# Fused matmul and row RMS norm on one core: the first loads reordered around the table load, the first moves split over two engines, eight warm matmuls instead of eleven

## The chip, the cores and the metric

The kernel runs on one core of a Trainium2 chip. The metric is the time of one execution in device microseconds, lower is better. "Span" is the time from the first to the last instruction in the profile; it is about 1.8 us less than the reported time.

The engines are called TensorE (PE in the profile, PEld for its weight loads), VectorE (DVE), ScalarE (ACT), GpSimd (POOL) and SyncE (SP). A "q" after the name (ACTq) is the engine's sequencer, which issues instructions and DMAs.

## The reference

```python
m, k, n = 2048, 2048, 2048          # a: [m, k], b: [k, n], gamma: [n], all float32

def reference(a, b, gamma, eps):
    x = np.matmul(a, b)
    rms = np.sqrt(np.mean(x ** 2, axis=-1, keepdims=True) + eps)
    return (gamma * x / rms).astype(np.float32)
```

## The kernel before

The contraction has 16 tiles of 128 rows, handled as eight pairs (kp = 0 to 7). In its head, the kernel forms the first four row blocks (HB = 4) times the left half of B, pair by pair: for each pair it needs a piece of A (512 rows by 256 columns) and a tile of B (256 rows by 1024 columns). Pair 0 comes as float32 on the two hardware DMA queues (SyncE and ScalarE) and is cast on the engines. Pairs 1 to 7 come through the software queue, which GpSimd feeds and which casts to bf16 on the way.

```python
    # pair 0, float32, on the hardware queues
    nc.sync.dma_start(out=a0f, in_=a[0:HB * P, 0:W2].rearrange("(r p) k -> p r k", p=P))
    for t in range(2):
        nc.scalar.dma_start(out=b0f[t], in_=b[t * P:(t + 1) * P, 0:HALF])
    # ... cut ...
    def load_head(kp):            # one pair through the software queue: A's piece, then B's tile
        nc.gpsimd.dma_start(out=ah(kp), in_=a[0:HB * P, kp * W2:(kp + 1) * W2].rearrange(...))
        load_b(0, kp)
    load_head(1)
    identity_f = consts.tile([P, P], FP32, name="identity_f")
    make_identity(nc, identity_f)
    for kp in range(2, 4):
        load_head(kp)
    # ... cut ...
    # warm matmuls: of zeros, only to keep TensorE busy until data is there
    warm_bank = ps_a.tile([P, CH], FP32, name="acc")
    for _ in range(11):
        nc.tensor.matmul(warm_bank, warm[:, 0:P], warm[:, 0:CH], start=True, stop=True)
    # ... cut ...
    def transpose_first():        # pair 0: transpose A on TensorE, move it out of PSUM, cast B
        bank = [ps_t.tile([P, CH], FP32, name="tbank"), ps_a.tile([P, CH], FP32, name="acc")]
        view = [b.rearrange("p (r m) -> p r m", r=HB) for b in bank]
        for t in range(2):
            for r in range(HB):
                nc.tensor.matmul(view[t][:, r, :], a0f[:, r, t * P:(t + 1) * P], identity_f,
                                 is_transpose=True, start=(r == 0), stop=(r == HB - 1))
        for t in range(2):
            cast_first = [lambda: nc.vector.tensor_copy(out=raw[0][0][:, t, :CH],
                                                        in_=b0f[t][:, :CH]),
                          lambda: nc.scalar.copy(out=raw[0][0][:, t, CH:], in_=b0f[t][:, CH:])]
            move = [lambda h=h: nc.vector.tensor_copy(
                out=head_at[:, t, 2 * h:2 * h + 2, :], in_=view[t][:, 2 * h:2 * h + 2, :])
                for h in range(2)]
            for work in (cast_first + move if t == 0 else move + cast_first):
                work()
```

After that each pair is 7 + 7 matmuls of 128x512, 8 transposes for the next pair and 2 matmuls into a separate bank. The rest of the kernel (right half of B, then Strassen products for the other row blocks, the norms and the stores) is not touched by the change.

## Time and profile before

| | before |
|---|---|
| time | 224.43 us, median of 3 (224.06 to 224.67) |
| span of the profiled run | 222.6 us |
| TensorE, busy share of the span | 95% |
| first matmul of pair 0 | 7.71 us |
| first matmul of pair 1 | 12.38 us |
| first matmul of pair 4 | 24.69 us |

First, the chain that ended last, from the profile's page of the kernel before: the shares of the span by engine.

```profile
PE 83%; DMA 8%; DVE 2%; POOL 2%; issue 1%; ACT 1%; DVEq 0%; ACTq 0%; POOLq 0%
```

The same chain in order of time (start us, us, what), where it passes from loads to TensorE:

```profile
6.53 0.65 POOL early L106
7.18 17.47 DMA b<-in_b_dram
24.64 0.04 issue
24.69 1.67 PE acc L350 x7
```

From 24.69 us on, the chain is TensorE until 209.5 us. What holds the start of that stretch is a load: B's tile for pair 4, issued at 7.18 us and landed at 24.64.

Next, lines of the timeline of the kernel before (start us, us of busy time, engine, line, operation, out<-in, count, and in brackets the idle time before it and what ended it):

```profile
0.74 0.46 SPq L92 DMA_DIRECT2D early<-in_a_dram  x1
0.75 0.91 ACTq L94 DMA_DIRECT2D early<-in_b_dram  x2
1.46 3.92 PE L138 MATMUL acc<-sq 128*128 128x512 bf16 x11 [1.46 <-DVE sq L129]
1.69 1.28 ACT L153 ACT_TABLE_LOAD   x1 [1.69 <-PEq L718]
...
5.14 0.73 DVE L151 CAST b<-early 128x512 bf16<-128x512 f32 x1 [1.32 <-DMA early<-in_b_dram]
...
6.57 0.63 PE L148 MATMUL tbank<-identity_f,early 128*128 128x128 f32 x4 [1.18 <-POOL msq L198]
7.23 0.76 DVE L154 CAST head_at<-tbank 128x256 bf16<-128x256 f32 x2 [1.36 <-PE tbank L148]
7.71 2.76 PE L350 MATMUL acc<-b,head_at 128*128 128x512 bf16 x12
10.31 0.61 PE L165 MATMUL tbank<-identity,early 128*128 128x128 bf16 x8
...
23.65 0.59 PE L382 MATMUL tbank<-b,head_at 128*128 128x512 bf16 x2
24.69 1.67 PE L350 MATMUL acc<-b,head_at 128*128 128x512 bf16 x7 [0.44 <-DMA b<-in_b_dram]
```

- VectorE casts B's first tile at 5.14 us, *before* A has landed. When the transposes are done, at 7.2, only the move out of PSUM is left, and the first matmul follows 0.48 us after the move starts.

- The last pair of lines shows slack. From pair 1 on, the two matmuls into the separate bank (L382) are followed 0.43 us later by the next pair, except before pair 4. There TensorE would have been ready at 23.65 + 0.43 = 24.08 us, and waited until 24.69: 0.6 us.

The landing records in the trace (a load is complete with its sixteenth increment, one from each DMA engine) suggest why: of pair 4's tile fifteen parts had landed by 23.68 us and the sixteenth at 24.64, 0.96 us later. A 16 KB packet of the instruction queue started at 21.38 us and took 0.97 us.

### The profile page before, as it was taken

The numbers are of one execution on the slowest core, as the hardware profiler recorded it, in microseconds if no ns is written. First come the engines' busy times: TensorE is split into PE (matmuls) and PEld (weight loads), VectorE is DVE, ScalarE is ACT, GpSimd is POOL, SyncE is SP. The second block draws the span as 40 slices with busy tenths as digits, with TensorE's granted clock in tenths as the row PEclk, the third lists the DMA queues.
The fourth block names the chain that finished last, engine by engine and source line by source line (L and its number), as shares of the span: only waits on it lengthen the run. The fifth ranks groups of instructions, "written<-read, shape, count | busy, mean of one in ns | idle before, by whom it ended". The sixth has DMA issues, their size and how long they took to land.

```text
span 222.6 us, 3026 instructions
## 1 busy us (share of the span) xinstructions
PE 211.1 (95%) x1043; PEld 98.6 (44%) x1043; DVE 161.8 (73%) x324; ACT 129.1 (58%) x272; POOL 24.5 (11%) x49
## 2 busy tenths in 40 slices
PE   7899999999999999999999999999999999999950
PEld 2445444444454444444444444444444444444430
DVE  2427557983999989978949298837994589587692
ACT  3110002807698895799646985699478954334570
POOL 7534232300000001000100002000200000000000
PEclk9999999999999999999999999999999999999997
DMA  6999999999973499818889259945994794044045
GB/s 184 223 202 209 203 208 211 212 303 259 327 280 159 188 272 292 310 72 226 276 228 400 58 174 222 366 151 143 246 368 168 97 282 189 0 188 193 0 190 188
DMA packets 36176, 47.13 MB, mean 212 GB/s; under 512 B 21952, under 2 KB 26048, under 8 KB 34496
## 3 DMA queue, kind: packets, MB, share of 16 engines
q0 software_dynamic: 9648, 23.33, 41.6%
q1 hardware_dynamic: 26080, 22.29, 33.0%
q10 hardware_dynamic: 432, 1.31, 2.0%
q8 instruction: 8, 0.13, 0.2%
q14 instruction: 8, 0.07, 0.1%
HBM read 34.60 MB, written 16.78 MB: 231 GB/s over the span
## 4 chain that ended last, share of the span: by engine, by line
PE 83%; DMA 8%; DVE 2%; POOL 2%; issue 1%; ACT 1%; DVEq 0%; ACTq 0%; POOLq 0%
PE acc L279 63%; PE acc L350 18%; DMA b<-in_b_dram 8%; POOL early L106 1%; DVE x L617 1%; POOL b L100 1%; DVE x L620 1%; PE tbank L179 1%; PE tbank L382 1%; PE tbank L165 1%; ACT sq L291 0%; DVEq L732 0%; ACT sq L682 0%; DVE x L690 0%; DVE r L322 0%
## 5 line engine op out<-in xcount | busy, mean ns | idle before, releaser
L279 PE MATMUL acc<-b,s 128*128 128x512 bf16 x376 | 83.3, 379 | 0.0
L279 PEld LDWEIGHTS <-s 128*128 128x128 f16 x472 | 46.2, 98 | 55.7 <-DVE s L244 0.2
L350 PE MATMUL acc<-b,head_at 128*128 128x512 bf16 x240 | 55.1, 379 | 0.6 <-DMA b<-in_b_dram 0.4
L291 ACT ACTIVATE sq<-x 128x512 bf16<-128x512 f32 x62 | 39.1, 631 | 10.9 <-DVE x L520 5.1
L340 DVE SCALAR_TENSOR_TENSOR x<-x,r,gamma_sb 128x1024 f32<-128x1024 f32 x28 | 34.7, 1282 | 0.8
L209 ACT ACTIVATE sq<-a 128x1024 bf16<-128x1024 f32 x24 | 25.4, 1057 | 16.8 <-DMA a<-in_a_dram 16.4
L350 PEld LDWEIGHTS <-head_at 128*128 128x128 bf16 x240 | 22.9, 98 | 26.7 <-issue 1.1
L393 ACT COPY x<-acc 128x512 f32<-128x512 f32 x11 | 5.9, 591 | 25.1 <-PE acc L350 25.1
L231 ACT ACTIVATE head_at<-a,s 128x2048 f16<-128x2048 f32 x10 | 19.9, 1990 | 0.0
L279 PEld LDWEIGHTS <-at_even 128*128 128x128 f16 x96 | 9.4, 98 | 11.5 <-issue 0.4
L279 PEld LDWEIGHTS <-head_at 128*128 128x128 f16 x96 | 9.4, 98 | 11.3
L100 POOL DMA_DIRECT2D b<-in_b_dram x15 | 10.6, 708 | 16.0 <-DMA b<-in_b_dram 13.2
L217 DVE TENSOR_SCALAR s<-norm 128x1 f32<-128x1 f32 x12 | 1.8, 150 | 14.3 <-ACT norm L212 14.2
L244 DVE TENSOR_TENSOR s<-at_even 128x1024 f16<-128x1024 f16 x15 | 9.7, 684 | 2.8 <-DMA at_even<-head_at 2.8
L291 ACT ACTIVATION_READ_ACCUMULATOR sq<-x 128x1 f32 x62 | 11.7, 188 | 0.0
L279 PE MATMUL acc<-t_left,s 128*128 128x512 bf16 x48 | 11.3, 379 | 0.0
L279 PE MATMUL acc<-early,s 128*128 128x512 bf16 x48 | 11.3, 379 | 0.0
L279 PE MATMUL acc<-early,at_even 128*128 128x512 bf16 x48 | 11.0, 379 | 0.0
L279 PE MATMUL acc<-t_left,at_even 128*128 128x512 bf16 x48 | 10.9, 379 | 0.0
L509 ACT COPY x<-acc 128x512 f32<-128x512 f32 x10 | 5.7, 575 | 8.9 <-PE acc L279 8.9
L279 PE MATMUL acc<-t_left,head_at 128*128 128x512 bf16 x48 | 10.8, 379 | 0.0
L279 PE MATMUL acc<-early,head_at 128*128 128x512 bf16 x48 | 10.8, 379 | 0.0
(86 smaller groups left out, 205.8 us busy)
## 6 DMA issues: line engine op xcount, KB each, us to landing
out_dram<-x SPq DMA_DIRECT2D x30, 512.0 KB, 3.1
a<-in_a_dram POOLq DMA_DIRECT2D x12, 1024.0 KB, 8.5
b<-in_b_dram POOLq DMA_DIRECT2D x15, 512.0 KB, 17.1
early<-in_a_dram POOLq DMA_DIRECT2D x7, 256.0 KB, 14.8
early<-in_b_dram ACTq DMA_DIRECT2D x2, 512.0 KB, 5.9
gamma_sb<-in_gamma_dram POOLq DMA_DIRECT2D x1, 1024.0 KB, 19.9
out_dram<-x SPq DMA_DIRECT2D x3, 256.0 KB, 3.5
early<-in_a_dram SPq DMA_DIRECT2D x1, 512.0 KB, 5.7
```

The source lines that it names most:

```text
L100: nc.gpsimd.dma_start(out=raw[j][kp], in_=b[kp * W2:(kp + 1) * W2, j * HALF:(j + 1) * HALF].rearrange("(t p) n -> p t n", p=P))
L106: nc.gpsimd.dma_start(out=ah(kp), in_=a[0:HB * P, kp * W2:(kp + 1) * W2].rearrange("(r p) k -> p r k", p=P))
L165: nc.tensor.matmul(view[:, t, r, :], ah(kp)[:, r, t * P:(t + 1) * P], identity, is_transpose=True, start=(t == 0 and r == 0), stop=(t == 1 ...
L209: nc.scalar.activation(out=junk, in_=a32[mb][:, h * HALF:(h + 1) * HALF], func=ACTF.Square, scale=2.0 ** -8, accum_out=n2[:, h:h + 1])
L231: nc.scalar.activation(out=a16[mb], in_=a32.pop(mb), func=ACTF.Copy, scale=factor.pop(mb))
L244: nc.vector.tensor_tensor(out=s_sum[s], in0=x, in1=y, op=op)
L279: nc.tensor.matmul(bank, lhsT[:, kp, :], rhs, start=(start and kp == 0), stop=(kp == KP - 1), skip_group_check=not start)
L291: nc.scalar.activation(out=sq[:, 0:CH], in_=src, func=ACTF.Square, scale=inv_sqrt_n, accum_out=msq[mb][:, c:c + 1])
L340: nc.vector.scalar_tensor_tensor(out=x, in0=x, scalar=r, in1=gamma_sb[:, h * HALF:(h + 1) * HALF], op0=ALU.mult, op1=ALU.mult)
L350: nc.tensor.matmul(bank, head_at[:, kt, r, :], head_rhs(c, kt), start=(kt == 0), stop=(kt == KT - 1))
L393: copy(out=x_chunk(*g), in_=banks[g])
L509: nc.scalar.copy(out=x21, in_=p2)
```

## The change

Its intent is to have A alone on one hardware queue, with B's two tiles behind a table load on the other, and to split the first moves out of PSUM over two engines. A tiny Sqrt on ScalarE pulls the activation table's load to the front (one load then serves the whole kernel; before there was a second at 53.6 us). With A expected earlier, three warm matmuls are dropped, and the move of A's first bank now stands ahead of the cast of B's first tile.

```diff
     nc.sync.dma_start(out=a0f, in_=a[0:HB * P, 0:W2].rearrange("(r p) k -> p r k", p=P))
+    pace = consts.tile([P, 1], FP32, name="pace")
+    nc.vector.memset(pace, 1.0)
+    nc.scalar.activation(out=pace, in_=pace, func=ACTF.Sqrt)
     for t in range(2):
         nc.scalar.dma_start(out=b0f[t], in_=b[t * P:(t + 1) * P, 0:HALF])
@@
-    pace = consts.tile([P, 1], FP32, name="pace")
@@
-    for _ in range(11):
+    for _ in range(8):
         nc.tensor.matmul(warm_bank, warm[:, 0:P], warm[:, 0:CH], start=True, stop=True)
@@
-        for t in range(2):
-            cast_first = [lambda: nc.vector.tensor_copy(out=raw[0][0][:, t, :CH],
-                                                        in_=b0f[t][:, :CH]),
-                          lambda: nc.scalar.copy(out=raw[0][0][:, t, CH:], in_=b0f[t][:, CH:])]
-            move = [lambda h=h: nc.vector.tensor_copy(
-                out=head_at[:, t, 2 * h:2 * h + 2, :], in_=view[t][:, 2 * h:2 * h + 2, :])
-                for h in range(2)]
-            for work in (cast_first + move if t == 0 else move + cast_first):
-                work()
+        copy = (nc.vector.tensor_copy, nc.scalar.copy)
+
+        def move(t):
+            for h in range(2):
+                copy[t](out=head_at[:, t, 2 * h:2 * h + 2, :], in_=view[t][:, 2 * h:2 * h + 2, :])
+
+        def cast(t, h):
+            copy[h](out=raw[0][0][:, t, h * CH:(h + 1) * CH], in_=b0f[t][:, h * CH:(h + 1) * CH])
+
+        move(0)
+        cast(0, 0)
+        cast(0, 1)
+        move(1)
+        cast(1, 0)
+        cast(1, 1)
```

## The prediction

> **What bounds the kernel now.** The chain of waits puts 83% of the 222.6 us span on TensorE and 8% on one load: B's tile for pair 4 of contraction tiles, landing at 24.64 us. After 24.69 TensorE never waits again until 209.5. So only what moves 24.69 can move the time. Before it, loads hold the kernel, not the first pair: in the timeline and the DMA landing records pair 1's B tile lands at 12.34 and its matmuls start at 12.38; later tiles land every 3.83 us (16.04, 19.87, then 24.64, 28.47, 32.29, 36.12) and TensorE needs 3.9 us per pair (starts 12.38, 16.28, 20.18, 24.69). Pair 4 lands 0.9 us late: one engine fetched instructions for 0.97 us at 21.4. TensorE would have been ready at 24.08, so its own path has 0.6 us of slack.
>
> **What the change does.** Before: SyncE issues A at 0.74, ScalarE both B tiles at 0.75 to 1.66, then loads its table (1.69, 1.28 us). The DMA packets by queue show B tile 0 moving from 1.8 to 4.5, A mostly from 3.5 to 6 behind it, B tile 1 from 5.5 to 8.3; landings A 6.43, B 5.12 and 8.67. First transposes 6.57, first real matmul 7.71. After: table load (about 0.8 to 2.1) and a tiny Sqrt (estimate 0.25) come first; B is issued near 2.35 and 2.8, first packets near 3.4. A has the engines alone: 0.52 MB at the 300 GB/s of 4.5 to 5.5 gives, as an estimate, landing at 4.0 to 4.8. Eight warm matmuls (427 ns each while slow) end near 4.9, just then. Transposes, moves (0.38 us each) split over two engines; B tile 0 lands near 6, tile 1 at 8.5 to 9.5. First real matmul near 6.7 to 7, 0.7 to 1 us earlier; pair 0's second half about as before. The second table load, near 50 us, goes (-1.28 us of ScalarE, off the path). The Trainium skill, "ScalarE: Activation LUTs", section "What ACT_TABLE_LOAD costs", gives 1283 ns; the trace agrees.
>
> **How much is on the path.** An earlier first matmul alone buys almost nothing: pair 1 still waits for its tile. The gain must come from the software queue running earlier. Issued from 1.25, its first packet moved at 6.38, 5.1 us later; the paced loads later in this kernel took 1.6 to 2.7 us. So I think it sat behind the two hardware queues, as the Trainium skill, "DMA: Bandwidth & Descriptors", section "Issuing engines are not separate DMA queues", leads one to expect: all queues share the same 16 engines. With B 1.6 us later, the software queue gets room near 3 us, and the early low rate (66 to 200 GB/s from 1.5 to 3.5, against 400 with two queues) is partly filled. Estimate: software tiles 0.3 to 1.2 us earlier, pair 4 at 23.4 to 24.3; but B tile 1, sharing engines, can be late and use up TensorE's slack. Net gain 0.1 to 0.9 us.
>
> **Prediction:** 224.0 us, 223.2 to 224.8 (before's three runs alone spread over 0.6). Faster by over 2%: 0.01; within 2%: 0.98; slower by over 2%: 0.01.
>
> **Right or wrong.** A lands before 4.9, first transpose near 5, first real matmul near 6.8; if A is still after 6, the premise on the queues is wrong. First software packet clearly before 6 and pair 1's B tile before 12: my cause of the gain; if both are unmoved, the time is unchanged although TensorE starts earlier. TensorE's unbroken stretch starts at 23.8 to 24.6 instead of 24.69, and from there everything lasts as long.
>
> **What would make it wrong.** The software queue's 5 us being start-up, not queueing (no gain); B tile 1 landing after 9.8 (a loss of tenths); the instruction fetch hitting another tile.

## More of the kernel before

- The eleven warm matmuls run into the time in which A is awaited. The trace's clock record gives TensorE its full clock from 4.29 us in this run.

## The result

| | before | after |
|---|---|---|
| time, median of 4 | 224.38 us (224.06 to 224.67) | 225.58 us (224.96 to 226.28) |
| ratio to before | | 1.0056, 95% interval 1.0034 to 1.0079 |
| span of the profiled run | 222.6 us | 223.2 us |
| full clock from | 4.29 us | 9.79 us |
| A landed; B's two tiles landed | 6.43; 5.12, 8.67 us | 6.21; 5.63, 8.88 us |
| first matmul of pair 0 | 7.71 us | 8.62 us |
| first matmul of pair 1 | 12.38 us | 13.59 us |
| first matmul of pair 4 | 24.69 us | 25.29 us |

Here and below, a ratio is the mean time of one kernel's runs over that of the other's runs in the same rounds, so it is not quite the ratio of the medians. Executions over 1.5% slower than the fastest of the same kernel are left out of the means. The change makes the kernel slower by half a per cent, 1.2 us at the median; the profiled run is the fastest of its four and only 0.6 us longer than before's. The spread has more than doubled.

The chain that ended last, from the page of the changed kernel: DMA's share is down from 8% to 2%, TensorE's is up from 83% to 90%.

```profile
PE 90%; DVE 3%; DMA 2%; ACT 1%; issue 0%; DVEq 0%; ACTq 0%
```

In order of time its beginning is now the first load of A and the work on pair 0 ("issue" pieces of 0.14 us and less left out):

```profile
0.74 5.47 DMA early<-in_a_dram
6.35 1.10 PE tbank L149 x4
7.47 0.76 DVE head_at L155 x2
8.23 0.34 DVE b L158
8.62 3.31 PE acc L357 x12
```

Lines of the changed kernel's timeline that answer to those shown of before:

```profile
0.74 1.28 ACT L95 ACT_TABLE_LOAD   x1 [0.74 <-PEq L725]
0.74 0.45 SPq L92 DMA_DIRECT2D early<-in_a_dram  x1
0.91 0.87 ACTq L97 DMA_DIRECT2D early<-in_b_dram  x2
1.49 3.60 PE L139 MATMUL acc<-sq 128*128 128x512 bf16 x8 [1.49 <-DVE sq L130]
2.03 0.20 ACT L95 ACTIVATE pace<-pace 128x1 f32<-128x1 f32 x1
...
6.35 1.09 PE L149 MATMUL tbank<-identity_f,early 128*128 128x128 f32 x4 [1.26 <-DMA early<-in_a_dram]
7.47 0.76 DVE L155 CAST head_at<-tbank 128x256 bf16<-128x256 f32 x2 [3.66 <-PE tbank L149]
8.15 0.42 DVE L158 CAST b<-early 128x512 bf16<-128x512 f32 x1
8.62 3.31 PE L357 MATMUL acc<-b,head_at 128*128 128x512 bf16 x12 [0.33 <-DVE b L158]
9.00 0.15 PEld L357 LDWEIGHTS <-head_at 128*128 128x128 bf16 x1 [0.28 <-issue]
...
11.77 0.61 PE L172 MATMUL tbank<-identity,early 128*128 128x128 bf16 x8
...
25.29 1.67 PE L357 MATMUL acc<-b,head_at 128*128 128x512 bf16 x7
```

Read against the kernel before:

- B is issued at 0.91 us, in the middle of the table load (0.74 to 2.02) and 1.1 us before the Sqrt that stands ahead of it in the program. B is not "behind" anything; A lands only 0.2 us earlier.
- The four transposes of a bank take 1.09 us instead of 0.63, and the weight loads of the first real matmuls take 0.15 us with 0.28 us gaps, the pace of the warm matmuls (one per 0.43 us). This is the slow clock; the full one came at 9.79.
- From the start of the first move to the first matmul it is now 1.15 us instead of 0.48: VectorE casts B's first tile after the moves, though the tile had landed at 5.63, before A.

Term by term up to the 8 transposes of pair 1 (10.31 before, 11.77 after, +1.46): transposes start 0.22 earlier; slow transposes delay the first move by 0.46 more (7.23 to 7.47 in spite of the earlier start); the order costs 1.15 − 0.48 = 0.67; the twelve matmuls take 11.77 − 8.62 = 3.15 instead of 2.60, 0.55 more. So about 1.0 us comes from the clock and 0.7 from the order. Pair 1 then starts 1.21 us later and pair 4 at 25.29, with no wait for its tile (landed at 23.89). Before it started at 24.69, but TensorE was ready at 24.08: half of the lateness disappears in the slack. That is the profiled run; the slower runs must have lost more somewhere.

### The profile page after: what moved, and what is told of

Same layout as the page of the kernel before. It is cut to its first block, busy times and chain, and to the rows that moved or that the text cites. A ratio compares the mean times of both kernels' runs of the same rounds, so it can differ in the third digit from the quotient of the medians.

```text
span 223.2 us, 3021 instructions
## 1 busy us (share of the span) xinstructions
PE 211.8 (95%) x1040; PEld 99.2 (44%) x1040; DVE 161.0 (72%) x323; ACT 128.5 (58%) x274; POOL 24.5 (11%) x49
## 4 chain that ended last, share of the span: by engine, by line
PE 90%; DVE 3%; DMA 2%; ACT 1%; issue 0%; DVEq 0%; ACTq 0%
PE acc L286 63%; PE acc L357 23%; DMA early<-in_a_dram 2%; PE tbank L389 2%; PE tbank L172 1%; DVE x L624 1%; DVE x L627 1%; PE tbank L186 1%; PE tbank L149 0%; ACT sq L298 0%; DVE head_at L155 0%; DVE head_at L177 0%; DVEq L739 0%; ACT sq L689 0%; DVE x L697 0%
```

## The experiments

All outputs are right. "Warm" is the number of warm matmuls.

### Eleven warm matmuls again: a_w11

```diff
-    for _ in range(8):          # on the changed kernel
+    for _ in range(11):
```

> The changed kernel with 11 warm matmuls again instead of 8; nothing else. Theory 1 (clock: the full TensorE clock came at 9.8 us in the changed kernel's trace against 4.3 in before's, because 8 matmuls keep TensorE busy too short): full clock by about 4.3 to 5, the 8 first transposes take 1.1 us in all again and not 1.9, first matmul near 8.3, pair 1 starts near 12.9 instead of 13.6; time 224.4 to 224.9, ratio to before 1.000 to 1.002. Theory 2 (order: VectorE's casts of B's first tile now stand behind the moves, 0.67 us): unchanged at 225.3 to 225.7, ratio 1.004 to 1.006. Theory 3 (loads: B lands 0.2 to 0.5 us later): unchanged too.

Measured: 224.26 us against 224.37 of before, ratio 0.9999 (0.9986 to 1.0011). Full clock from 7.17 us, pair 1 at 12.90. Three lines of its timeline:

```profile
1.49 4.87 PE L139 MATMUL acc<-sq 128*128 128x512 bf16 x11 [1.49 <-DVE sq L130]
6.22 1.08 PE L149 MATMUL tbank<-identity_f,early 128*128 128x128 f32 x4
8.49 2.75 PE L357 MATMUL acc<-b,head_at 128*128 128x512 bf16 x12 [0.74 <-DVE b L158]
```

The whole loss is gone with this one number. The warm matmuls now run until A is there (no idle before the transposes at 6.22), the first transposes are still slow, but the twelve matmuls are fast (2.75). The clock came later than I expected (7.17, not 5), and it was early enough. The wait for VectorE's cast is still there, 0.74 us, and pair 1 is still 0.5 us late; it costs nothing.

### Eight in the kernel before: b_w8

```diff
-    for _ in range(11):         # on the kernel before
+    for _ in range(8):
```

> The kernel before with 8 warm matmuls instead of 11; nothing else. Theory 1 (clock): full clock only after 9 us, pair 1 starts near 13.0 to 13.3 instead of 12.38; time 224.7 to 225.2, ratio 1.002 to 1.004. Theories 2 (order) and 3 (loads): nothing changes, ratio 0.999 to 1.001, pair 1 at 12.4.

Measured: 224.84 us, ratio 1.0022 (1.0008 to 1.0035): in the range that the clock theory gave, but its profiled run does not show the reason that it gave. In that run the full clock came at 4.77 us all the same, and pair 1 started at 12.31. What was late was pair 4's tile: the instruction packet started at 22.79 instead of 21.38 us, and the tile's last part landed at 24.85, after TensorE had waited for it:

```profile
24.89 1.67 PE L350 MATMUL acc<-b,head_at 128*128 128x512 bf16 x7 [0.72 <-DMA b<-in_b_dram]
```

The packet's time goes with the number of warm matmuls: 21.35 to 21.47 us in the six profiles with eleven, 22.79 to 24.51 with eight, 23.91 to 25.56 with four (b_hwheld, a_w4 and the two kernels with B held left out). So eight warm matmuls do not always lose the clock, and the profile alone explains 0.2 us of the 0.5.

### The casts first again: a_castfirst

```diff
+        cast(0, 0)              # on the changed kernel
+        cast(0, 1)
         move(0)
-        cast(0, 0)
-        cast(0, 1)
         move(1)
```

> The changed kernel with the casts of B's first tile ahead of the moves again, still 8 warm matmuls and the moves on two engines. Theory 2 (order): first matmul near 8.2 instead of 8.62, pair 1 near 13.1; time 224.9 to 225.3, ratio 1.002 to 1.004. Theory 1 (clock) alone: unchanged, ratio 1.004 to 1.006, full clock still after 9 us. Theory 3 (loads): unchanged.

Measured: 225.27 us, ratio 1.0040 (1.0027 to 1.0052). In the profiled run the full clock came at 10.86, and all loads were 0.4 to 0.5 us later than in the changed kernel's first trace (A at 6.74). The order may be worth 0.3 us here, but the interval overlaps that of the changed kernel. Undoing the order does not cure it.

### Both undone: a_w11_castfirst

> Both undone: 11 warm matmuls and the casts of B's first tile first; what stays of the change is the table load ahead of B's issue and the moves of the second transposed bank on ScalarE. If theories 1 and 2 together are the cause: first matmul near 7.6, pair 1 at 12.4 to 12.5, time 224.0 to 224.5, ratio 0.998 to 1.001. Theory 3 (loads landing 0.2 us later for good): ratio 1.003 or more.

Measured: 224.29 us, ratio 0.9999 (0.9987 to 1.0012); first matmul at 7.92, later than the 7.6 expected; full clock from 7.07. With eleven warm matmuls the order makes no difference (224.26 and 224.29).

### B's issue made to wait: a_realwait and a_realwait_w11

```diff
+    for t in range(2):          # on the changed kernel
+        nc.scalar.activation(out=b0f[t][:, 0:1], in_=pace, func=ACTF.Sqrt)
     for t in range(2):
         nc.scalar.dma_start(out=b0f[t], in_=b[t * P:(t + 1) * P, 0:HALF])
```

The loads overwrite the column that ScalarE has written, so they must wait for it.

> The changed kernel made to do what its words say: ScalarE writes one column of each B tile with a Sqrt after the table load, and the B loads, which overwrite it, must wait for that write. Still 8 warm matmuls. If A is late because B shares the engines with it (intent of the change; my prediction): B issued near 2.7, first B packet near 3.7, A lands at 3.8 to 4.9 instead of 6.2, first transpose at about 5.1 right behind the warm matmuls, full clock before 7.5, B tile 1 lands at 9 to 9.6, time 223.9 to 224.7. If A's own path is slow: A still lands after 5.8. If the software queue waits behind the hardware queues, its first packet comes clearly before 6 (near 3); if its 5 us are its own start-up, again at 6.3 to 6.8.

> The same with 11 warm matmuls. If A lands by 4.9 the three more warm matmuls only delay the transposes (to about 5.8 to 6.2); full clock by 7.5 at the latest; time 223.9 to 224.6, within 0.1% of the kernel before. A time above 225 would mean that late B tiles and not the clock decide.

Measured: 228.88 us, ratio 1.0191 (1.0167 to 1.0214), and with eleven warm matmuls 228.12, ratio 1.0176 (1.0150 to 1.0202). Both missed their expectations (at most 224.7 and 224.6) by 3.5 us and more, and the second is above the 225 us that was to mean that late B tiles and not the clock decide. Lines of the first one's timeline:

```profile
2.50 0.87 ACTq L99 DMA_DIRECT2D early<-in_b_dram  x2
4.57 0.60 PE L151 MATMUL tbank<-identity_f,early 128*128 128x128 f32 x4
...
11.24 0.62 ACT L160 CAST b<-early 128x512 bf16<-128x512 f32 x1 [8.68 <-DMA early<-in_b_dram]
11.80 4.06 PE L359 MATMUL acc<-b,head_at 128*128 128x512 bf16 x12 [6.19 <-DVE b L160]
```

The intent works up to a point: A alone landed at 4.21 us, and the transposes ran at 4.57, right behind the warm matmuls. But B's first tile landed at 11.22 and the second at 13.51. The queues of this run from 6 to 6.5 us (q10 is ScalarE's hardware queue with B, q0 the software queue: packets, MB, share of 16 engines) tell where the engines' time went:

```profile
q10 hardware_dynamic: 17, 0.07, 49.9%
q0 software_dynamic: 24, 0.04, 41.0%
```

and the same half microsecond in the kernel before (q1 is SyncE's hardware queue, with A):

```profile
q10 hardware_dynamic: 30, 0.12, 85.8%
q1 hardware_dynamic: 3, 0.00, 1.3%
q0 software_dynamic: 1, 0.00, 0.7%
```

The software queue, whose first packet moved at 3.23 us here instead of 6.38, takes two fifths of the engines' time, and B, which pair 0 needs first, is left with half. And nothing comes back later: pair 4's tile landed at 25.23 us, 0.6 later than before. In this run the order moved the lateness from one load to another and shortened nothing; that the total of the 16 engines is what is short fits this and is not shown. TensorE, idle from 5.6 to 11.8, also lost its full clock at 7.65 and got it back at 14.47.

### The software queue alone: b_hwheld

```diff
     make_identity(nc, identity_f)          # on the kernel before
+    nc.vector.tensor_copy(out=a0f[:, 0, 0:1], in_=identity_f[:, 0:1])
+    for t in range(2):
+        nc.vector.tensor_copy(out=b0f[t][:, 0:1], in_=identity_f[:, 0:1])
+    # A's load on SyncE and B's two on ScalarE now stand here
```

> A look at the software queue's start alone: the kernel before with all three hardware loads held until the identity is built (about 3.5 us), so that the software queue has the 16 engines to itself from its first issue at 1.25. Slower by 2 to 3 us on purpose. If the software queue sat behind the hardware queues: its first packet at 2.8 to 4.0. If it needs 5 us to start by itself: first packet at 6.0 to 6.8 here too.

Measured: one look, 234.18 us. The software queue from 2.5 to 3 us in this run:

```profile
q0 software_dynamic: 11, 0.01, 52.4%
```

Its first packet moved at 2.83 us, 1.6 after its issue. So the 5.1 us in the kernel before were queueing and not start-up, as the prediction held. The reverse shows too: the hardware loads, issued at 3.64 and 3.71 us, moved their first packets at 8.27 and 8.58, 4.6 us or more later, and landed at 12.3 to 15.3. In these runs a load issued behind others waited for much of what was ahead of it, on either kind of queue. It was far slower than the 2 to 3 us that I had expected.

### B's second tile on SyncE: a_w11cf_b1sync

```diff
-        nc.scalar.dma_start(out=b0f[t], in_=...)      # on a_w11_castfirst
+        (nc.scalar, nc.sync)[t].dma_start(out=b0f[t], in_=...)
```

> A candidate: 11 warm matmuls and the casts first, and B's second tile issued on SyncE behind A, so that both hardware queues carry data till the end (one alone moved about 230 GB/s from 6 to 8 us, both together 400). If a single queue's pace is the limit: tile 1 lands near 7.5 instead of 8.7 to 9.1, pair 1's B tile 0.5 to 1 us before 12.3, time 223.3 to 224.0. If the engines' total is the limit or the loads are taken in order of issue: tile 1 lands at 8.5 to 9.2 as before and the time is 224.2 to 224.5.

Measured: 224.49 us, ratio 1.0000 (0.9987 to 1.0014); the tile landed at 8.98. That rules out, for this tile, the pace of one queue as the limit. This was the candidate for a version that beats both kernels, and it does not.

### Each part alone on the kernel before: b_order and b_table

> The kernel before with only the new order and engines of the first moves and casts (11 warm matmuls, B's issue ahead of the table load). If a lateness of TensorE of up to 0.6 us is hidden behind the load of pair 4 (my theory now): first matmul near 8.3 to 8.5 instead of 7.71, pair 1 at 12.8 to 13.0, pair 4 still starts with its tile at 24.4 to 24.8, ratio 0.999 to 1.001. Rival: the order counts in full, +0.5 us, ratio 1.002 to 1.003.

> The kernel before with only the early table load and tiny Sqrt ahead of B's issue. If the issue is done by a sequencer that runs ahead of the engine: B is issued at about 0.9 to 1.3 in spite of the table load up to 2.02, landings A 6.0 to 6.7, B tiles 5.4 to 6.1 and 8.7 to 9.3, ratio 0.999 to 1.002. If the table load did hold the issue: B first packet after 3, as where it was made to wait, and A before 4.5.

Measured: b_order (the new order and engines of moves and casts) 224.37 us, ratio 1.0001 (0.9990 to 1.0013); b_table (the early table load and the tiny Sqrt) 224.41, ratio 1.0005 (0.9993 to 1.0017). Two lines of b_order's timeline and two of b_table's:

```profile
8.25 2.75 PE L356 MATMUL acc<-b,head_at 128*128 128x512 bf16 x12 [0.74 <-DVE b L157]
...
24.72 1.67 PE L356 MATMUL acc<-b,head_at 128*128 128x512 bf16 x7 [0.20 <-DMA b<-in_b_dram]
```

```profile
0.74 1.28 ACT L95 ACT_TABLE_LOAD   x1 [0.74 <-PEq L720]
...
0.91 0.88 ACTq L97 DMA_DIRECT2D early<-in_b_dram  x2
```

With the new order the first matmul is 0.54 us late, and the wait before pair 4 shrinks instead: 0.20 us of waiting is left of 0.44. The slack pays. (The first matmul and pair 1, at 12.66, came a little earlier than expected.) In b_table the issue at 0.91 goes past the table load as in the changed kernel, and A and B land within 0.7 us of before.

### A clock that is late in every run: b_w4, and the changed kernel again: a_again

```diff
-    for _ in range(11):         # b_w4, on the kernel before
+    for _ in range(4):
```

> The kernel before with 4 warm matmuls[...]: full clock only from 9.3 to 12.8 in every run (mean clock 0.982 to 0.988). Clock theory: TensorE reaches pair 1 at 13.0 to 13.7 and pair 4 at 24.7 to 25.4, time 224.7 to 225.5, ratio 1.001 to 1.005, without any change of order or loads. If the clock does not matter: ratio 0.999 to 1.001.

> The changed kernel itself once more, for the spread of its clock and times beside the three above on one chip: ratio 1.004 to 1.007; the runs with the lower mean clock (0.982 to 0.984) at 225.5 to 226.3, one with 0.988 or more at 224.8 to 225.3, as in its first four runs. If the time did not follow the clock from run to run, the clock theory would be weaker.

Measured: b_w4 225.75 us (225.63 to 225.94), ratio 1.0064 (1.0052 to 1.0076). Full clock from 11.60 us, the twelve matmuls took 4.41 us of busy time instead of 2.76, pair 1 at 14.32, pair 4 at 26.02:

```profile
8.26 4.41 PE L350 MATMUL acc<-b,head_at 128*128 128x512 bf16 x12
...
26.02 1.67 PE L350 MATMUL acc<-b,head_at 128*128 128x512 bf16 x7
```

No load and no order was changed: a late clock alone can cost what the change cost. It cost even more than expected (224.7 to 225.5 us, pair 4 by 25.4); the repeat below gave 225.25 us.

a_again: 225.60 us (224.05 to 226.59), ratio 1.0054 (1.0026 to 1.0082), a repeat of the first result. Its profiled run (224.84 us) is the early case of the same program: full clock from 5.44 us, and then

```profile
6.44 0.63 PE L149 MATMUL tbank<-identity_f,early 128*128 128x128 f32 x4 [1.35 <-POOL msq L205]
...
8.25 2.75 PE L357 MATMUL acc<-b,head_at 128*128 128x512 bf16 x12 [0.74 <-DVE b L158]
...
25.11 1.67 PE L357 MATMUL acc<-b,head_at 128*128 128x512 bf16 x7 [0.59 <-DMA b<-in_b_dram]
```

Here TensorE was in time and the load of pair 4 was not: as in b_w8 the instruction packet came later (23.00), fifteen parts of the tile were there at 23.80 and the sixteenth at 25.07.

Both expectations used the runs' mean clock, and that was a mistake. The clock record starts when the full clock is granted, so the mean leaves out the slow start: before's 0.993 is (215.04 at full + 3.28 at half) over the 218.3 us from 4.29 to the end. A run cannot be sorted into early and late by it, and a_again's slowest run had 0.992. A low mean tells something else. Of the profiled fast runs only a_realwait (0.975) and a_realwait_w11 (0.983) have one below 0.987, and in both the full clock was granted, lost for two steps and one step of 3.41 us, and granted again. Five of the changed kernel's ten runs have means of 0.982 to 0.984 and took 225.55 to 226.28 us. So half of its runs probably got the full clock early and lost it in the gaps of the head; no profile fell on one, and this stays an inference. With the casts first and eight warm matmuls such means are rarer (a_castfirst one run in five, b_w8 none in five).

### Late clock with either order: a_w4, a_w4_castfirst, and two repeats

All with four warm matmuls; a_w4 is the changed kernel otherwise, a_w4_castfirst has its casts first.

> The changed kernel with 4 warm matmuls, so that the late clock comes in every run and not by chance. If the changed kernel's time is a mixture of early and late clocks plus an order cost that shows only once the slack of 0.6 us is gone: 226.0 to 226.6 with a spread under 0.6, at the slow end of the changed kernel's own runs (224.05 to 226.59), ratio 1.008 to 1.010; that is 0.3 to 0.8 us above the kernel before with 4 warm matmuls (225.75), though the same new order cost nothing with 11. If the order is free throughout: 225.6 to 225.9, ratio 1.006.

> The same with the casts of B's first tile first again. If the order costs once the slack is gone: 0.3 to 0.6 us less than with 4 warm matmuls and the new order, 225.5 to 225.9, ratio 1.005 to 1.007, the level of the kernel before with 4. If the order is free: equal to it within 0.1.

> The kernel before with 4 warm matmuls, unchanged, a second time, now beside the next one on the same chip. If chance (the phase of the clock's control, landings a few tenths earlier or later) made the gap of 1.0 us between it (225.75) and the changed kernel with 4 warm matmuls and the old cast order (224.73): the two are within 0.5 us of each other now, both between 224.6 and 225.8. If the early table load and the moves on two engines are worth 1 us when the clock is late: again 225.6 to 225.9.

> The changed kernel with 4 warm matmuls and the casts first, unchanged, a second time. Chance: within 0.5 us of the run above, 224.6 to 225.8. A real gain of table load and two engines with a late clock: again 224.6 to 224.9 and 0.8 us or more under the run above.

| kernel | runs, us | ratio | 95% interval |
|---|---|---|---|
| a_w4 | 225.12 to 226.53 | 1.0062 | 1.0042 to 1.0081 |
| a_w4_castfirst | 224.54 to 225.22 | 1.0010 | 0.9997 to 1.0024 |
| b_w4_again | 224.62 to 225.85 | 1.0036 | 1.0017 to 1.0056 |
| a_w4_castfirst_again | 224.65 to 226.14 | 1.0052 | 1.0034 to 1.0070 |

One execution of a_w4, the profiled one (258.80 us at a mean clock of 0.853), is left out. The expectations missed here: a_w4 spread over 1.4 us, not under 0.6, and a_w4_castfirst was first 1 us better than b_w4 and in the repeat no better. So that gap was chance from one execution or chip to the next, and four warm matmuls do not fix a level. Within one call, the new order was 0.5% slower than the old (a_w4 against a_w4_castfirst); the repeat of the latter, on another chip, is within 0.1% of a_w4. Whether the order costs its full 0.67 us once the slack is used up is likely from the traces, and not settled by the times.

## Why the prediction was wrong

**What all traces say together.** The table has the profiled runs (a_w4's left out, being slow, and b_hwheld's). "Tile" is when pair 4's B tile was complete, "start" the first matmul of pair 4, "rest" the span minus that start.

| kernel | warm | full clock from | pair 1 start | tile | start | span | rest |
|---|---|---|---|---|---|---|---|
| before | 11 | 4.29 | 12.38 | 24.64 | 24.69 | 222.61 | 197.92 |
| b_table | 11 | 4.63 | 12.50 | 24.49 | 24.53 | 222.60 | 198.07 |
| b_order | 11 | 4.12 | 12.66 | 24.68 | 24.72 | 222.82 | 198.10 |
| a_w11 | 11 | 7.17 | 12.90 | 24.43 | 24.59 | 222.46 | 197.87 |
| a_w11_castfirst | 11 | 7.07 | 12.73 | 24.55 | 24.59 | 222.52 | 197.93 |
| a_w11cf_b1sync | 11 | 4.86 | 12.60 | 24.87 | 24.91 | 222.79 | 197.88 |
| b_w8 | 8 | 4.77 | 12.31 | 24.85 | 24.89 | 222.80 | 197.91 |
| a_again (changed) | 8 | 5.44 | 12.66 | 25.07 | 25.11 | 223.04 | 197.93 |
| after (changed) | 8 | 9.79 | 13.59 | 23.89 | 25.29 | 223.19 | 197.90 |
| a_castfirst | 8 | 10.86 | 14.14 | 24.30 | 25.84 | 223.73 | 197.89 |
| b_w4 | 4 | 11.60 | 14.32 | 23.84 | 26.02 | 223.93 | 197.91 |
| b_w4_again | 4 | 10.96 | 13.99 | 23.80 | 25.69 | 223.63 | 197.94 |
| a_w4_castfirst | 4 | 10.42 | 13.60 | 23.62 | 25.30 | 223.21 | 197.91 |
| a_w4_castfirst_again | 4 | 12.06 | 14.75 | 24.33 | 26.45 | 224.36 | 197.91 |
| a_realwait | 8 | 4.23, lost 7.65, 14.47 | 17.51 | 25.23 | 29.21 | 227.10 | 197.89 |
| a_realwait_w11 | 11 | 6.71, lost 10.12, 13.54 | 16.27 | 24.96 | 27.97 | 225.89 | 197.92 |

The rest is 197.9 to 198.1 us in all of them. The start of pair 4 is the whole story, and it is the later of two things: the tile (rows with an early clock start 0.04 to 0.05 us after it) or TensorE's own path (a_w11, 0.16 us after its tile, and all rows with a late or lost clock).

**Point by point.**

- *"Only what moves 24.69 can move the time"*: right, shown by the column "rest".
- *"Table load and a tiny Sqrt come first; B is issued near 2.35 and 2.8"*: **this is the step that failed.** B was issued at 0.91 us in the changed kernel and in b_table, during the table load. The Trainium skill, "Perfetto Trace Analysis", section "Sequencer Loop", has what fits: the sequencer pushes an engine instruction into a queue for engine instructions, and it is there that the instruction waits. The DMA issue stands in this trace as the sequencer's (ACTq), and the table load did not hold it. I had taken program order on one engine for order in time. This took away the forecast gain (b_table, 1.0005; and with B really held there was none either, a_realwait, 1.0191); the loss came from the step on the warm matmuls below, which rested on it.
- *"A lands at 4.0 to 4.8"; "first real matmul near 6.7 to 7"*: wrong, 6.21 and 8.62, for that reason. Where B was really held, A landed at 4.21 (a_realwait): the estimate was good and its premise false.
- *"Eight warm matmuls end near 4.9, just then"*: the time was right (8 matmuls from 1.49, busy for 3.60 us), the "just then" was not. A came 1.1 us later, and TensorE stood idle from 5.1 to 6.35. I did not ask what that gap does to the clock. The Trainium skill, "TensorE: Matmul & The Clock Gate", section "Part 1: The HAM clock gate", says that a free-running window of 3413 ns decides. The traces agree: between the grant and the later drop of the full clock there are 215.04, 211.63 or 208.21 us, steps of 3.41 us, so both lie on one grid, and the grid lies differently in each execution.

  TensorE's busy time in each window of these grids, over all profiles but a_w4's slow one, separates the cases: at half clock, every window with 2.66 us or more (b_order, 1.46 to 4.12) was followed by the full clock and none with 2.55 or less (a_castfirst, to 4.04); at full clock, windows with 1.37 us or less lost it (a_realwait, to 7.65) and those with 1.45 or more (a_again, near the end) kept it. An estimate from these numbers: eight matmuls, busy from 1.49 to 5.09, put 2.66 us into one window only if it ends between 4.15 and 5.84 us, about half of the positions of the grid.

  With eight warm matmuls and a gap, the profiled grants came at 4.77, 5.44, 9.79 and 10.86 us; with eleven, never after 7.2 (kernels with loads held left out). The smaller number of warm matmuls made the clock a matter of chance. That it made the loss is shown (a_w11: gone with eleven); that the clock is how it did so, and made the wider spread, is shown in the profiled runs and inferred for the others, the slowest (226.28, 226.59) among them.
- *"Moves split over two engines"*: I costed the moves and overlooked that the cast of B's first tile was put behind them: 0.67 us on TensorE's path. With eleven warm matmuls it costs nothing (b_order 1.0001), because the wait before pair 4 pays. In the changed kernel it uses up that slack before the clock's lateness arrives.
- *"The software queue sat behind the hardware queues"*: right, b_hwheld. *"Its earlier start fills the early low rate, software tiles 0.3 to 1.2 us earlier"*: wrong. In the change itself it did not start earlier (first packet 6.48), and where it did (a_realwait, 3.23) pair 4's tile came 0.6 us later. *"B tile 1, sharing engines, can be late"* named the right danger: in a_realwait, B landed at 11.2 and 13.5 us and the loss was ten times larger than "a loss of tenths". In the change itself B landed at 8.88 and this was not the cause.
- *"The instruction fetch hitting another tile"*: right as a risk, seen in both directions. In the late runs it comes after pair 4's tile (at 24.06 in the changed kernel) and spares it; in b_w8 and a_again it comes at 22.8 and 23.0 and delays it by 1.2 to 1.3 us against the other fifteen parts.

**What stays open.** How much of the 1.2 us is the order when the clock is late (times between 0 and 0.5% of difference), and the loads: with the early table load A landed anywhere from 6.09 to 6.83 us, without it from 6.31 to 6.43, and no run tells why.

No version beat both kernels. The traces show why the head had little to give: the tiles of pairs 1 to 7 land about every 3.8 us and TensorE needs 3.9 us for a pair, and pair 1's tile landed at 12.2 to 12.9 us in all kernels whose loads were not held. Only b_hwheld had it earlier (9.96), and there pair 0's loads were late.

## What to carry to other kernels

Here a DMA issue that stood behind an engine instruction in the program did not wait for it (issued at 0.91 us, the table load ended at 2.02); if it is meant to wait, it needs a data dependency (a_realwait: issued at 2.50), and then one must ask who takes the engines in the meantime. Let warm-up work last until the real work begins: here a gap of 1.3 us left the clock to chance, and it showed as a wider spread rather than as one clear cost. Before counting on an earlier start, look for the next wait behind it, here pair 1's tile and pair 4's tile: the same slack hid a delay of half a microsecond in one variant and was missing in the next.

## What the Trainium skill lacked or had wrong

- "TensorE: Matmul & The Clock Gate", Part 1: the full clock is said to come after at least one busy window of about 3.4 us. A partly busy window was enough here: the full clock came 2.66 us after the first warm matmul (b_order, 1.46 to 4.12 us) and 2.83 us in the kernel before, while 2.55 us of busy time in a window was not enough (a_castfirst). The grid of 3.41 us agrees.
- "DMA: Bandwidth & Descriptors", section "Queues, rings and completion order": each engine is said to go round the queues packet by packet. Once all are moving, the runs agree roughly (a_realwait, 6 to 6.5 us: 17 packets of B and 24 of the software queue). At the start no such turns are seen, and the page does not say why: the software queue's first packet moved 5.1 us after its issue behind the hardware loads, against 1.6 us alone, and in the reverse order the hardware loads' first packets moved 4.6 us after issue.
- The same page, "Latency and other measured facts": a first byte after about 1 us (software) and 0.6 us (hardware). From the start of the issue to the first packet with free engines it was 1.6 us (b_hwheld) and 1.06 us (before, 0.75 to 1.81); from the end of the issuing instruction 0.7 us (2.13 to 2.84) and 0.63 us (1.18 to 1.81). The page does not say from where it counts.
- "Runtime: NRT & Kernel Launch", section "Instruction fetch mechanics": crossing a 16 KB boundary is called mostly hidden. Here a packet of 16 KB took 0.97 us while the loads needed the engines, and the last part of the tile in flight came 0.96 us after the other fifteen (kernel before); that the one made the other is inferred.
- "Perfetto Trace Analysis", section "Sequencer Loop", lets one conclude that a DMA issue can overtake engine instructions ahead of it, but does not say so outright. Here it was issued at 0.91 us, 1.1 us before the Sqrt ahead of it began.
